# State stores moved from GpSimd's queue to SyncE's, three granules behind the update, with the values of the recurrent samples loaded two steps ahead

## The chip, the cores and the metric

The kernel runs on one core of one Trainium2 chip. The metric is the device time of one execution in microseconds; the figure for the kernel before is the median of three runs. Engines are named as in the profile: PE (TensorE matmul), PEld (its weight load), DVE (VectorE), ACT (ScalarE), POOL (GpSimd) and SP (SyncE). SP and GpSimd appear here mostly as queues from which transfers (DMAs) are issued.

## The reference, cut to what matters

One layer of a decoder trunk runs over 256 prompt tokens and 8 single-token samples, 264 columns in all. An input projection feeds three mixers (A: spatial gating, B: HGRN2, C: gated linear attention); their outputs are projected, gated, merged and projected again, and a squared-ReLU MLP follows. All of it is float32. The change touches the part of mixers B and C that belongs to the samples. Each sample has a recurrent state per head, which is read, updated by its one token and written back, and whose product with the query is the mixer's output:

```python
# per sample b and head h; B has 8 heads of 128x128, C has 4 heads of 128x256
S_new = exp(log_f)[:, None] * S_old + k[:, None] * v[None, :]   # written out
o     = S_new.T @ q                                              # used further on
```

The three groups of the kernel are heads 0 to 3 of B, heads 4 to 7 of B, and the four heads of C. Each has 8 samples, so 8 steps of four heads in B's groups and 16 steps of two heads in C's; each step's state is 256 KB.

## The kernel before, in words

The matrix work is a long row of *granules*. A granule (`granule`) takes 512 KB of weights from SP's queue (`Stream.load`, line 613), splits them into a high and a low part (`split`: ACT casts `whi` on line 109, DVE subtracts for `wlo` on line 106), and multiplies three times per weight tile (lines 656, 657, 658: `whi` by high, `whi` by low, `wlo` by high), 24 matmuls in all. Weights are loaded five granules ahead into four `raw` buffers and split two ahead into six half-granule buffers.

After each granule `background()` counts `now[0]` up by one and lets two queues of Python generators go on: `bg` (the mixers' prompt part, `mixer_r`) and `bs` (the samples' part, `samples_r`), the latter at half a step a granule. A generator yields a cost, or a condition that must hold before it goes on. Products that PE owes for either of them are gathered and issued in a *slot* (`slot`), between two granules: `levels` (line 678) for the prompts and `samples` (line 685) for the states. `Rounds.load` (line 339) loads the weights of the modulation on SP, and `Rounds.steps` (line 376) uses them.

`samples_r` goes through the steps of a group. `fetch` loads a state into one of four `st` buffers (line 1081, GpSimd), `values` loads the sample's value rows, broadcast over 128 partitions, from a small DRAM tile `vs_d` into one of two `vbc` buffers (line 1087, GpSimd). Then ACT scales the state (line 1107), DVE adds the outer product (line 1109), and GpSimd stores it (line 1110). The state stays in its buffer until the slot has used it. In step n the program issues, in this order, the fetch of step n+2, the values of step n+1, the update of step n, and its store.

What sets the order on each engine: in this stage PE's and GpSimd's instructions run in the order in which the program emits them (`manual_schedule`), while a scheduler orders those of ACT, DVE and SP beforehand and may move work ahead of its place in the program. On the chip every engine runs its own list in order, and an instruction that waits holds up all behind it on that engine.

At the group's end the rows `os_` are normalised (lines 1119 to 1121); `finish` transposes them on PE (line 1307) where the mixer's output is needed. `A1` and `A2`, `G1` and `G2` are small tiles of modulation factors, each used in a stage of its own.

Of the kernel before, what the change touches and what calls it, by code (L numbers as in the profile page):

```python
# [15 lines left out]
P = 128  # L16
D = 2048
KT = D // P
# [3 lines left out]
NC = 1 + NS  # L22
# [13 lines left out]
CHUNKS = (2, 2, 4, 4, 4)  # L36
RATES = ((1.8, 0.5), (1.6, 0.5), (1.25, 0.5), (1.0, 0.5))
ST_BUFS = 4
VB_BUFS = 2
N_PRE = 6  # L40
PRE_AT = (2, 3, 4)
ADA_BATCH = 4
# [15 lines left out]
def hybrid_step_kernel(  # L58
# [8 lines left out]
    nc = tc.nc  # L67
# [14 lines left out]
    def nm(s):  # L82
        uid[0] += 1
        return f"{s}_{uid[0]}"

    def blk(shape=None, dt=F32):
        shape = shape or [P, 4, NT]
        return blkp.tile(shape, dt, tag="b", name=nm("b"))
# [4 lines left out]
    def tmp(shape, tag, bufs=2):  # L93
        return tp.tile(shape, F32, tag=tag, name=nm(tag), bufs=bufs)

    def const(shape, name, dt=F32):
        return cp.tile(shape, dt, tag=name, name=name)

    def mul(o, a, b):
        V.tensor_tensor(o, a, b, op=ALU.mult)  # L100
# [25 lines left out]
    order = tc.manual_schedule(engines={mybir.EngineType.PE, mybir.EngineType.SP, mybir.EngineType.Pool})  # L126
# [263 lines left out]
    now = [0]  # L390
# [78 lines left out]
    A1 = const([P, KT, NC], "A1")  # L469
# [190 lines left out]
                done(acc0)  # L660
        stream[0].ahead()

    levels, samples = [], []

    def slot():

        lv = [x for x in levels if x[0] + AGE <= now[0]][:2]
        sv = [x for x in samples if x[0] + AGE <= now[0]]
        del levels[:len(lv)]
        del samples[:len(sv)]  # L670
        if lv:
            pl = sm([P, 2, 8, 32])
            for i, (_, lhs, rhs, _) in enumerate(lv):
                for h in range(4):
                    for hf in range(2):
                        for b in range(4):
                            t0 = hf * P + b * 32
                            T.matmul(pl[32 * b:32 * b + 32, i, 2 * h + hf, :], lhs[:, h, t0:t0 + 32], rhs[:, h, t0:t0 + 32], start=True, stop=True)  # L678
        if sv:
            G, qm, os_ = sv[0][1]  # L680
            nh = 512 // G.dv
            po = sm([P, G.dv])
            for h in range(4):
                for i, (_, _, b, sts) in enumerate(sv):
                    T.matmul(po[32 * h:32 * h + 32, :], qm[:, h, b, :], sts[h // nh][:, h % nh, :], start=i == 0, stop=i == len(sv) - 1)  # L685
        if rounds.due():
            rounds.steps()
        for i, (_, _, _, put) in enumerate(lv):
            put(pl[:, i])
        if sv:  # L690
            if sv[0][2] == 0:
                V.tensor_copy(os_, po)
            else:
                add(os_, os_, po)
# [3 lines left out]
    def background():  # L698

        now[0] += 1  # L700
        while later and later[0][0] < now[0]:
            later.pop(0)[1]()
        bg.pump(rate[0])
        bs.pump(rate[1])
        wait = max([now[0] + 1 - AGE - x[0] for x in levels + samples] + [0])
        if wait and any(x[1][0].i == 2 for x in samples):
            wait += 2
        if rounds.due() and (wait or now[0] >= rounds.at + rounds.pace) or wait >= SLOT_WAIT:
            slot()
        rounds.tick()  # L710
# [13 lines left out]
    def tiles(bl):  # L724
        return lambda k: moving(bl[k // 4][:, k % 4, :])

    def pair(b, g):
        return b[:, 2 * g:2 * g + 2, :]
# [57 lines left out]
    order = tc.manual_schedule(engines=set(every))  # L786
# [97 lines left out]
    def mixer_a():  # L884
# [71 lines left out]
        for gp in range(4):  # L956
# [12 lines left out]
            )  # L969
            V.scalar_tensor_tensor(u[:, :, 0:NP], yv[:, :, 0:NP], 0.5, u[:, :, 0:NP], ALU.mult, ALU.mult)  # L970
            yield
    order = tc.manual_schedule(engines={mybir.EngineType.PE, mybir.EngineType.Pool})
    order.__enter__()
    gen_a = mixer_a()
    bg.g.append(gen_a)
# [56 lines left out]
    def gla_group():  # L1032
# [30 lines left out]
        G.gates = gates  # L1063
        return G

    def samples_r(G):

        dv = G.dv
        nj, nh = dv // P, 512 // dv
        q, k, g = G.q, G.k, G.g  # L1070
        fs = tmp([P, 4, NS], "fs")
        S.activation(fs, g[:, :, NP:NT], AF.Exp)
        qm = blk([P, 4, NS, 32])
        mul(qm, q[:, :, NP:NT].unsqueeze(3).to_broadcast([P, 4, NS, 32]),
            delta.rearrange("p (b c) -> p b c", b=NS).unsqueeze(1).to_broadcast([P, 4, NS, 32]))
        steps = [(b, h) for b in range(NS) for h in range(0, 4, nh)]
        ahead, vals = [], []

        def fetch(b, h):
            st = tmp([P, nh, dv], "st", ST_BUFS)  # L1080
            nc.gpsimd.dma_start(st, G.s_in(b, h, nh))
            ahead.append((st, now[0]))

        def values(b, h):
            v = tmp([P, 4, P], "vbc", VB_BUFS)
            r0 = 4 * nj * b + h * nj
            nc.gpsimd.dma_start(v, vs_d[G.i, r0:r0 + 4, :].partition_broadcast(P))
            vals.append((v.rearrange("p (h j) v -> p h (j v)", h=nh), now[0]))

        for s in steps[0:2]:  # L1090
            fetch(*s)
            yield
        values(*steps[0])
        yield
        os_ = tmp([P, dv], f"os{G.i}", 1)
        sts = []
        for n, (b, h0) in enumerate(steps):
            if n + 2 < len(steps):

                yield lambda: len(sts) + sum(len(x[3]) for x in samples) <= ST_BUFS - 3  # L1100
                fetch(*steps[n + 2])
            if n + 1 < len(steps):
                values(*steps[n + 1])
            yield lambda: now[0] >= max(ahead[0][1] + FETCHED, vals[0][1] + FETCHED - 1)
            st, v = ahead.pop(0)[0], vals.pop(0)[0]
            for i in range(nh):
                S.activation(st[:, i, :], st[:, i, :], AF.Copy, scale=fs[:, h0 + i, b:b + 1])  # L1107
            for i in range(nh):
                V.scalar_tensor_tensor(st[:, i, :], v[:, i, :], k[:, h0 + i, NP + b:NP + b + 1], st[:, i, :], ALU.mult, ALU.add)  # L1109
            nc.gpsimd.dma_start(G.s_out(b, h0, nh), st)  # L1110
            sts.append(st)
            if h0 + nh == 4:
                samples.append((now[0], (G, qm, os_), b, sts))
                sts = []
            yield
        yield lambda: not samples
        yield READY
        ss, rr = tmp([P, 1], "sss", 1), tmp([P, 1], "srr", 1)
        S.activation(tmp([P, dv], "vt"), os_, AF.Square, accum_out=ss)
        rstd_small(ss, 1.0 / dv, rr)  # L1120
        S.activation(os_, os_, AF.Copy, scale=rr)
        G.os = os_
        yield

    def mixer_r(G):
# [18 lines left out]
        q, k, g = G.q, G.k, G.g  # L1144

        bs.g.append(samples_r(G))


# [258 lines left out]
    G1 = const([P, KT, NC], "G1")  # L1407
# [41 lines left out]
    def put_rows(m, pt, rows):  # L1449
        S.copy(in_rows(rows, 0, m), pt[:, 0])  # L1450
        V.tensor_copy(in_rows(rows, 1, m), pt[:, 1])
# [20 lines left out]
    order = tc.manual_schedule(engines={mybir.EngineType.PE})  # L1472
# [7 lines left out]
    for m in range(8):  # L1480
        if m in PRE_AT:
            n = N_PRE // len(PRE_AT)
# [8 lines left out]
            S.activation(tmp([P, 1], "srr", 1), sqacc[:, 0:1], AF.Sqrt)  # L1491
    rounds.drain()
    rounds = pre
    A2 = const([P, KT, NC], "A2")
    V.scalar_tensor_tensor(A2, mod[:, 4 * KT:5 * KT, :], 1.0, gpre2T.unsqueeze(2).to_broadcast([P, KT, NC]), ALU.add, ALU.mult)
    B2 = mod[:, 3 * KT:4 * KT, :]
    order.__exit__(None, None, None)
    order = tc.manual_schedule(engines={mybir.EngineType.PE, mybir.EngineType.DVE, mybir.EngineType.Activation})
# [35 lines left out]
    Q.tensor_tensor(xsT, xsT, gs, op=ALU.add)  # L1534
    Q.tensor_tensor(xa, xsT, A2[:, :, 1:NC], op=ALU.mult)

# [50 lines left out]
    def put_quad(q, i2, i, src, vt):  # L1587
        k = 4 * q + 2 * i2 + i
        if i == 0 and (q == 0 or i2 == 0):
            V.tensor_scalar(vt[:, i, 0:NP], src, A2[:, k, 0:1], B2[:, k, 0:1], ALU.mult, ALU.add)  # L1590
        else:
            S.activation(vt[:, i, 0:NP], src, AF.Identity, scale=A2[:, k, 0:1], bias=B2[:, k, 0:1])
        if q == 0 or i == 1:
# [6 lines left out]

    rate[:] = (0.0, 0.0)
    rounds.pace, rounds.batch = 5, 2
    G2 = const([P, KT, NC], "G2")
    h2H, h2L = tiles(h2h), tiles(h2l)

    def begin_up():
# [33 lines left out]
    def down(f, ah, al):  # L1640
        for m in range(8):
# [8 lines left out]
            if f == NFB - 1:  # L1650
                g = gated(m, dst, G2)
                later.append((now[0], lambda m=m, g=g: put_rows(m, to_tokens(g), yt)))
# [3 lines left out]
    order = tc.manual_schedule(engines={mybir.EngineType.PE})  # L1656
    order.__enter__()
    pend = up(0, zs)
    for f in range(NFB):
        nxt = up(f + 1) if f + 1 < NFB else None  # L1660
        if f == NFB - 1:
            rounds.drain()
            mul(G2, mod[:, 5 * KT:6 * KT, :], gpost2T.unsqueeze(2).to_broadcast([P, KT, NC]))
            yt = [[blk([P, 1024]) for _ in range(2)] for _ in range(2)]
# [9 lines left out]
    order = tc.manual_schedule(engines=set(every))  # L1674
# [9 lines left out]
    dst = pair(y2[3], 1)  # L1684
# [3 lines left out]
    def last_tile(i):  # L1688
# [120 lines left out]
```

## Time and profile before

| | |
|---|---|
| Median of three runs | 1823.93 us (1821.64 to 1825.94) |
| The profiled execution | 1821.87 us |
| Its span, first to last instruction | 1820.0 us |
| Mean granted TensorE clock | 0.998 |
| PE busy | 1780.2 us (98%) |
| PEld busy | 1689.8 us (93%) |
| DVE busy | 1178.7 us (65%) |
| ACT busy | 996.9 us (55%) |
| POOL busy | 136.9 us (8%) |
| DMA, mean over the span | 243 GB/s |

The states are worked on between 356 us (first fetch) and 808 us (last product of a state) of the span. In the rows shown below, a group's row gives engine, line, operation, tiles and count; a row of the timeline begins with start and duration in microseconds and ends, in brackets, with the idle time of the engine before it and what ended that; a row of waits reads "who <- for whom: us in total, times, longest". A row of windows gives the stretch, its length, then the busy time of PE, PEld, DVE, ACT and POOL with the number of instructions, then the granted clock (1.00 is full), the DMA engines' busy share and GB/s.

### The profile page before, as it was taken

How to read it: one execution, taken by the hardware profiler on the slowest of the kernel's cores; microseconds unless marked ns; L12 is line 12 of the kernel's file. 1: busy time of each engine (PE TensorE's matmuls, PEld its weight loads, DVE VectorE, ACT ScalarE, POOL GpSimd, SP SyncE). 2: the span in 40 equal slices, each digit the busy share in tenths (PEclk: the TensorE clock that was granted, in tenths of full speed). 3: DMA queues.
4: the chain of work that ended last, by engine and by line, in shares of the span. 5: the costliest groups of instructions: out<-in, count | busy, mean ns of one | idle time of the engine just before them, and what ended most of it. 6: DMA issues, size and time to landing. Idle time of an engine off the chain costs nothing.

```text
span 1820.0 us, 42083 instructions
## 1 busy us (share of the span) xinstructions
PE 1780.2 (98%) x16970; PEld 1689.8 (93%) x16970; DVE 1178.7 (65%) x2077; ACT 996.9 (55%) x1824; POOL 136.9 (8%) x228
## 2 busy tenths in 40 slices
PE   6999999999999999999999999999999999999998
PEld 4889999989988989989999989999999999999998
DVE  4666567787577696566555667555666666666666
ACT  5444364676766766654445666555554545454544
POOL 3221000102111111210000000000000000000000
PEclk9999999999999999999999999999999999999999
DMA  9987788788788789897978954777666666666663
GB/s 325 339 348 262 253 282 261 211 257 290 231 290 264 227 271 301 274 321 243 307 248 267 330 168 152 251 256 223 195 196 194 195 196 196 197 196 193 196 193 118
DMA packets 330180, 442.05 MB, mean 243 GB/s; under 512 B 14947, under 2 KB 276945, under 8 KB 329985
## 3 DMA queue, kind: packets, MB, share of 16 engines
q1 hardware_dynamic: 311872, 380.52, 65.1%
q0 software_dynamic: 17184, 57.85, 9.0%
q8 instruction: 133, 2.18, 0.5%
q10 hardware_dynamic: 928, 0.99, 0.2%
q14 instruction: 63, 0.51, 0.1%
HBM read 427.60 MB, written 11.70 MB: 241 GB/s over the span
## 4 chain that ended last, share of the span: by engine, by line
PE 88%; DVE 2%; issue 2%; DMA 1%; ACT 1%; POOL 0%; ACTq 0%; DVEq 0%; POOLq 0%
PE mm L656 27%; PE mm L658 26%; PE mm L657 26%; PE ada L376 3%; DMA vbc<-vs_d 1%; PE ada L308 1%; PE sm L854 1%; DVE wlo L106 1%; PE sm L678 1%; PE sm L685 0%; DVE b L106 0%; PE sm L1578 0%; PE sm L1209 0%; DMA st<-in_state_hgrn_dram 0%; ACT whi L109 0%
## 5 line engine op out<-in xcount | busy, mean ns | idle before, releaser
L656 PE MATMUL mm<-b,whi 128*128 128x264 f32 x4608 | 1286.9, 279 | 6.8 <-ACT whi L109 2.5
L658 PE MATMUL mm<-b,wlo 128*128 128x264 f32 x4608 | 1274.5, 277 | 5.2 <-DVE wlo L106 4.8
L657 PE MATMUL mm<-b,whi 128*128 128x264 f32 x4608 | 1273.4, 276 | 0.5 <-DVE b L106 0.4
L106 DVE TENSOR_TENSOR wlo<-raw,whi 128x512 fp32r<-128x512 f32 x1136 | 768.8, 689 | 443.8 <-ACT whi L109 442.4
L109 ACT CAST whi<-raw 128x512 fp32r<-128x512 f32 x1136 | 688.9, 616 | 626.9 <-DVE wlo L106 310.7
L656 PEld LDWEIGHTS mm<-b,whi 128*128 128x128 f32 x4608 | 872.3, 189 | 48.7 <-issue 26.4
L658 PEld LDWEIGHTS mm<-b,wlo 128*128 128x128 f32 x4608 | 872.3, 189 | 7.1 <-DVE wlo L106 7.1
L657 PEld LDWEIGHTS mm<-b,whi 128*128 128x128 f32 x4608 | 872.4, 189 | 1.1 <-DVE b L106 0.6
L103 DVE TENSOR_TENSOR b<-b,mm 128x528 f32<-128x528 f32 (+1 forms) x137 | 95.4, 698 | 63.3 <-PE mm L658 55.6
L1109 DVE SCALAR_TENSOR_TENSOR st<-vbc,b,st 128x128 f32<-128x128 f32 (+1 forms) x96 | 34.2, 392 | 52.4 <-DMA vbc<-vs_d 45.9
L1107 ACT ACTIVATE st<-st,fs 128x128 f32<-128x128 f32 (+1 forms) x96 | 37.0, 430 | 48.2 <-DMA st<-in_state_hgrn_dram 28.2
L1746 POOL TENSOR_TENSOR gs<-b,G 128x16 f32<-128x16 f32 x1 | 0.2, 222 | 714.1 <-DVE b L103 714.1
L485 POOL DMA_DIRECT2D b<-in_w_ada_dram x64 | 46.3, 725 | 48.0 <-PE ada L308 30.4
L376 PE MATMUL ada<-araw,cT 128*32 128x512 f32 x296 | 40.7, 601 | 0.0
L308 PE MATMUL ada<-b,cT 128*32 128x256 f32 (+1 forms) x640 | 35.0, 355 | 5.3 <-DMA b<-in_w_ada_dram 5.3
L100 DVE TENSOR_TENSOR b<-b,b 128x512 f32<-128x512 f32 (+1 forms) x47 | 34.0, 743 | 1.3 <-ACT b L1221 1.0
L308 PEld LDWEIGHTS ada<-b,cT 128*32 128x32 f32 x640 | 17.8, 113 | 17.4 <-DMA b<-in_w_ada_dram 9.6
L1110 POOL DMA_DIRECT2D out_dram<-st x32 | 23.5, 735 | 129.5 <-DVE st L1109 129.5
L376 PE MATMUL ada<-b,cT 128*32 128x512 f32 x216 | 26.2, 593 | 0.0
L106 DVE TENSOR_TENSOR b<-gt,b 128x528 fp32r<-128x528 f32 x32 | 22.7, 711 | 3.2
L106 DVE TENSOR_TENSOR b<-b,b 128x1056 fp32r<-128x1056 f32 (+3 forms) x21 | 20.9, 993 | 5.9 <-ACT b L109 5.9
L106 DVE TENSOR_TENSOR b<-b 128x1024 f32<-128x1024 f32 (+1 forms) x24 | 24.3, 1018 | 0.0
(360 smaller groups left out, 895.8 us busy)
## 6 DMA issues: line engine op xcount, KB each, us to landing
raw<-in_w_in_dram SPq DMA_DIRECT2D x231, 512.0 KB, 5.0
raw<-in_w_mlp_up_dram SPq DMA_DIRECT2D x128, 512.0 KB, 3.9
raw<-in_w_mlp_down_dram SPq DMA_DIRECT2D x128, 512.0 KB, 3.7
araw<-in_w_ada_dram SPq DMA_DIRECT2D x74, 512.0 KB, 5.7
b<-in_w_ada_dram SPq DMA_DIRECT2D x54, 512.0 KB, 6.4
b<-in_w_ada_dram POOLq DMA_DIRECT2D x48, 512.0 KB, 11.3
raw<-in_w_branch_dram SPq DMA_DIRECT2D x48, 512.0 KB, 4.6
raw<-in_w_out_dram SPq DMA_DIRECT2D x32, 512.0 KB, 5.1
```

Of the source, the lines that this page charges most:

```text
L100: V.tensor_tensor(o, a, b, op=ALU.mult)
L103: V.tensor_tensor(o, a, b, op=ALU.add)
L106: V.tensor_tensor(o, a, b, op=ALU.subtract)
L109: S.copy(hi, src)
L308: T.matmul(acc[32 * j:32 * j + 32, 0:n], cT[:, k, :], w[:, n * j:n * j + n], start=k == 0, stop=k == KT - 1)
L376: T.matmul(self.acc[32 * j:32 * j + 32, :], cT[:, k, :], ws[j // 2][:, j % 2 * 512:j % 2 * 512 + 512], start=k == 0, stop=k == KT - 1)
L485: queue.dma_start(w[:, i], w1[k * P:(k + 1) * P, :, self.k0 * P:(self.k0 + self.n) * P])
L656: T.matmul(o, a, xh(k + j), start=first and j == 0, stop=False)
L657: T.matmul(o, a, xl(k + j), start=False, stop=False)
L658: T.matmul(o, b, xh(k + j), start=False, stop=last and j == n - 1)
L1107: S.activation(st[:, i, :], st[:, i, :], AF.Copy, scale=fs[:, h0 + i, b:b + 1])
L1109: V.scalar_tensor_tensor(st[:, i, :], v[:, i, :], k[:, h0 + i, NP + b:NP + b + 1], st[:, i, :], ALU.mult, ALU.add)
```

## The change

The stores of the states leave GpSimd's queue. They are put on a list with the granule at which they fall due, three after the update, and `background()` issues them from SP; a fetch that needs a buffer whose store is not yet issued issues that store first. SP's order in this stage is now the program's too. Values are loaded two steps ahead like the states, right behind the state of the same step, into three `vbc` buffers; both first steps' values are loaded before the loop, which adds one step of the generator. A group's end also waits until its stores are issued. To make room, the rows of the first two groups share one tile with the third group's, and `A2` and `G2` take the tiles of `A1` and `G1`.

```diff
-VB_BUFS = 2
+STORE_LAG = 3
+VB_BUFS = 3
...
     def background():
         now[0] += 1
+        while stores and stores[0][0] <= now[0]:
+            stores[0][2]()
         while later and later[0][0] < now[0]:
...
-    order = tc.manual_schedule(engines={mybir.EngineType.PE, mybir.EngineType.Pool})
+    order = tc.manual_schedule(engines={mybir.EngineType.PE, mybir.EngineType.Pool, mybir.EngineType.SP})
...
+        def store():
+            _, dst, st = out.pop(0)
+            nc.sync.dma_start(dst, st)
+            stores.pop(0)
...
-        values(*steps[0])
-        yield
-        os_ = tmp([P, dv], f"os{G.i}", 1)
-        sts = []
+        for s in steps[0:2]:
+            values(*s)
+            yield
+        if G.i != 1:
+            os_rows.append(tmp([P, 256], "os2", 1))
+        os_ = os_rows[-1][:, G.i % 2 * P:G.i % 2 * P + dv]
+        sts, out = [], []
         for n, (b, h0) in enumerate(steps):
             if n + 2 < len(steps):
                 yield lambda: len(sts) + sum(len(x[3]) for x in samples) <= ST_BUFS - 3
+                while out and out[0][0] <= n - 2:
+                    store()
                 fetch(*steps[n + 2])
-            if n + 1 < len(steps):
-                values(*steps[n + 1])
+                values(*steps[n + 2])
...
-            nc.gpsimd.dma_start(G.s_out(b, h0, nh), st)
+            out.append((n, G.s_out(b, h0, nh), st))
+            stores.append((now[0] + STORE_LAG, n, store))
...
-        yield lambda: not samples
+        yield lambda: not samples and not out
...
-    A2 = const([P, KT, NC], "A2")
+    A2 = A1
...
-    G2 = const([P, KT, NC], "G2")
+    G2 = G1
```

More of the change, by code (lines that the diff above doesn't have):

```diff
@@ L661, in granule @@
         stream[0].ahead()
-    levels, samples = [], []
+    levels, samples, stores = [], [], []
     def slot():
@@ L1064, in gla_group @@
         return G
+    os_rows = []
     def samples_r(G):
```

## The prediction

> **What bounds the kernel now.** The page comes first, then the waits of PE in the stage that the change touches (340 to 820 us), then the places of those waits.
>
> ```profile
> span 1820.0 us, 42083 instructions
> ...
> PE 88%; DVE 2%; issue 2%; DMA 1%; ACT 1%; POOL 0%; ACTq 0%; DVEq 0%; POOLq 0%
> ```
>
> ```profile
> PE mm L658 <- DVE wlo L106: 4.6, 5, 2.8
> PE sm L678 <- issue: 2.8, 2, 2.2
> PE mm L656 <- ACT whi L109: 1.8, 1, 1.8
> PE mm L656 <- ACT att L1187: 1.3, 1, 1.3
> ```
>
> TensorE carries 88% of the chain that ended last, and the change gives it not one matmul less. Only its idle time in this stage can be won, and the second fence holds all of it: 4.6 + 2.8 + 1.8 + 1.3 = 10.5 us. PE waits there for the weights' halves (`whi` from ACT, `wlo` from DVE), so the question is what kept those two engines. Three places of PE's timeline:
>
> ```profile
> 397.58 0.38 PE L656 MATMUL mm<-b,whi 128*128 128x264 f32 x1 [1.75 <-ACT whi L109]
> ...
> 398.51 0.59 PE L658 MATMUL mm<-b,wlo 128*128 128x264 f32 x1 [0.43 <-DVE wlo L106]
> ...
> 797.48 0.50 PE L658 MATMUL mm<-b,wlo 128*128 128x264 f32 x1 [2.78 <-DVE wlo L106]
> ```
>
> At 395.83 PE ran dry for 1.75 + 0.43 = 2.18 us, at 794.70 for 2.78 us. What ACT, DVE and GpSimd did before the first:
>
> ```profile
> 396.03 0.98 ACT L1107 ACTIVATE st<-st,fs 128x128 f32<-128x128 f32 x3 [8.91 <-DMA st<-in_state_hgrn_dram]
> ...
> 396.97 0.88 DVE L1109 SCALAR_TENSOR_TENSOR st<-vbc,b,st 128x128 f32<-128x128 f32 x3 [6.11 <-DMA vbc<-vs_d]
> ```
>
> ```profile
> 359.53 0.56 POOL L1087 DMA_DIRECT2D vbc<-vs_d  x1
> 388.30 0.76 POOL L1110 DMA_DIRECT2D out_dram<-st  x1 [28.22 <-DVE st L1109]
> 389.05 0.75 POOL L1081 DMA_DIRECT2D st<-in_state_hgrn_dram  x1
> 389.80 0.55 POOL L1087 DMA_DIRECT2D vbc<-vs_d  x1
> ```
>
> GpSimd stood 28.22 us at the store of step 0, since its update was not done. Behind the store were queued the state of step 3 (issued 389.05) and the values of step 2 (389.80). ACT, in its own order, stood 8.91 us at that state, DVE 6.11 us at those values; nothing was split meanwhile, and PE ran dry. The second place, as the chain of waits shows it:
>
> ```profile
> 788.41 0.44 POOL out_dram L1110
> ...
> 789.12 2.58 DMA vbc<-vs_d
> ...
> 795.95 0.48 DVE st L1109
> ```
>
> The values of the last step left at 789.12, behind the store of the step two before, and DVE's update began at 795.95. A stall costs twice, as the windows right behind the two places show (PE busy with its count first, granted clock sixth):
>
> ```profile
> 398.20:401.70 3.50, 3.19 (x14) 3.19 (x15) 3.47 (x7) 3.15 (x6) 0.00 (x0) 0.51 0.59 166
> 401.70:405.00 3.30, 3.30 (x32) 3.30 (x31) 3.30 (x7) 3.30 (x7) 0.00 (x0) 1.00 1.03 400
> ...
> 797.60:801.00 3.40, 3.40 (x16) 3.40 (x17) 3.40 (x6) 1.76 (x3) 0.26 (x1) 0.50 0.76 223
> ```
>
> The clock is granted at half for 3.4 us after each (16 matmuls in 3.40 us, where the middle row has 32 in 3.30), which loses 1.7 us each time.
>
> **The change part by part.**
>
> *Values two steps ahead, GpSimd without stores.* In all three groups DVE waits for values:
>
> ```profile
>   DVE st L1109: 45.9, 18
> ...
> DMA to landing us min/median/max: 3.9/6.3/8.3
> ```
>
> The 45.9 us are the ceiling on DVE's side; PE felt little of it. First place: state 3 has a free buffer, and values 2 have the third one, so both leave at about 360, beside the load at 359.53. The 8.91 and the 6.11 us go. What is late next: values 3, which need the buffer of update 0, whose end releases GpSimd at 388.30. They leave then instead of 389.80, 1.5 us before today's values 2, and land at the pace of today's (389.80 to 396.97, 7.2 us) at 395.5. If the scheduler of DVE's order puts update 3 where update 2 stands today, PE restarts 1.5 us earlier than at 398.51, at 397.0, and 397.0 - 395.8 = 1.2 us of the 2.18 stay. If it puts it later, nothing stays. I take the upper bound, 1.2, since DVE's order is not in the change's hands. For the clock the bounds are 0 and 1.7; I take 0, by the row of another gap, 2.19 us long, behind which the clock stayed whole:
>
> ```profile
> 672.61 0.53 PE L678 MATMUL sm<-b 128*32 128x32 f32 x37 [2.19 <-issue]
> ```
>
> Second group, the same wait:
>
> ```profile
> 517.95 0.61 DVE L1109 SCALAR_TENSOR_TENSOR st<-vbc,b,st 128x128 f32<-128x128 f32 x2 [5.77 <-DMA vbc<-vs_d]
> ```
>
> ```profile
> 519.84 0.38 PE L658 MATMUL mm<-b,wlo 128*128 128x264 f32 x1 [0.39 <-DVE wlo L106]
> ...
> 525.33 0.38 PE L658 MATMUL mm<-b,wlo 128*128 128x264 f32 x1 [0.40 <-DVE wlo L106]
> ```
>
> 0.79 us in all; 1.5 us earlier is enough to clear both. Last place: the values of step 15 of the third group now need only update 12 and their turn behind the fetch of state 15:
>
> ```profile
> 774.96 0.88 DVE L1109 SCALAR_TENSOR_TENSOR st<-vbc,b,st 128x256 f32<-128x256 f32 x2 [0.50 <-DMA vbc<-vs_d]
> ```
>
> ```profile
> 782.93 0.57 POOL L1087 DMA_DIRECT2D vbc<-vs_d  x1
> ```
>
> Update 12 ended at 775.8, and 782.93 is where today's values 14 stand, right behind that fetch. So they can go at 782.93 instead of 789.12, 6.2 us earlier: more than the 2.78 us gap, which goes with its 1.7 us of clock.
>
> *Stores on SP, three granules behind.*
>
> ```profile
> out_dram<-st POOLq DMA_DIRECT2D x32, 256.0 KB, 5.5
> ...
> out_dram<-b SPq DMA_DIRECT2D x5, 256.0 KB, 2.3
> ```
>
> ```profile
> L613 SPq DMA_DIRECT2D raw<-in_w_in_dram x191: 367/368/842, 18.1 to 965.2; - x191
> ```
>
> ```profile
> SPq L613 <- DVE wlo L106: 257.2, 101, 8.3
> ```
>
> 32 issues at 0.368 us are 12 us of SP, which spends 257.2 us of this stage waiting for splits: hidden. Without that cover they would cost at most 12 us. Each store waits on SP for its update, and the weight loads are queued behind it. But a granule is 24 matmuls, 2.5 us at the middle row's rate, and the load ahead of the store on SP already waits for a split that comes after the update in program order; so I take 0, against up to 8.3 us, the longest that SP stands today, of which PE would feel what its split buffers do not cover. The bytes are the same; in SP's ring a store can delay the load behind it by about 2.3 us (its own landing row), within that 8.3.
>
> *SP's order by hand.* Loads of the modulation weights, which the scheduler now pulls forward, come at their place in the program. Same loads, same bytes: 0, with the extra waits inside the bound just named.
>
> *One more step before each group, and the group's end also waits for its stores.* At half a step a granule that is two granules, 5 us.
>
> ```profile
> L1121 ACTq EVENT_SEMAPHORE  x2: 17/17/17, 620.0 to 813.4; - x2
> ```
>
> ```profile
> L1307 PE MATMUL sm<-cst,os x4: 272/272/273, 633.2 to 850.8; 128*128 128x128 f32 x4
> ```
>
> The second and third group's rows are ready at 620 and 813 and are transposed at 633 and 851: 13 and 37 us of cover, 0. *Shared tiles (`A1`, `G1`, the groups' rows)*: the new writers come after the old readers in both orders, 0.
>
> The sum: 2.18 + 2.78 + 0.79 of gaps and 2 x 1.7 of clock are 9.15 us won, 1.2 given back: 7.95. The profiled execution took 1821.87 (span 1820.0), so 1813.9; the median of the runs is 1823.93, 2.06 more, so **1816**.
>
> **The rivals.**
>
> *The state is late instead (slower).* A fetch needs its buffer's old store landed. GpSimd used to store right after the update; SP does so three granules later. The third group's fetches go in pairs, and the odd one's store comes out about when the slot's matmuls do:
>
> ```profile
> ACT st L1107 <- DMA st<-in_state_gla_dram: 13.7, 8, 2.8
> ```
>
> ```profile
> 772.37 0.88 DVE L1109 SCALAR_TENSOR_TENSOR st<-vbc,b,st 128x256 f32<-128x256 f32 x2 [7.22 <-DMA vbc<-vs_d]
> ```
>
> ```profile
> 779.28 0.64 PE L685 MATMUL sm<-st,b 128*32 128x256 f32 x8
> ```
>
> ```profile
> 784.38 0.37 SPq L613 DMA_DIRECT2D raw<-in_w_in_dram  x1
> ```
>
> The update of 772.37 would be stored behind the load of 784.38, land at 787 to 790 (2.3 or 5.5 us) and hold back the next fetch, which now goes right after the slot of 779.28, by 5 to 8 us; ACT would stand at that state, and so would the values behind it. ACT's 8.91 us cost PE 2.18, so 6.7 us are covered. Today's longest wait there is 2.8; a delay over 3.9 us decides. For it: the arithmetic of this pair. Against: 784.38 is late because DVE stood 7.22 us, which goes, and the scheduler that orders ACT knows of the lag. Each such stall costs what the first place costs, 2.18 + 1.7 = 3.9 us. One leaves 4.05 us of gain (1819.9), two leave 0.15 (1823.8), three make it 3.75 us slower (1827.7), four 7.65 (1831.6).
>
> *The engines of the DMA are the limit, not the order of issue.* Then values issued earlier land no earlier, and it stays at 1823.9. Against: values take 6.3 us from issue at the median whether somebody waits or not. The Trainium skill, "DMA: Bandwidth & Descriptors", section "Issuing engines are not separate DMA queues", holds that DMAs from SP and GpSimd share the same 16 engines, so a second issuer saves only issue time; by that rule the move by itself brings nothing. The trace agrees as to the bytes, but the wait of 28.22 us stands in front of an issue.
>
> *The half clock is not the stalls' doing.* Then 3.4 us of the gain stay lost: 1823.93 - 4.55 = 1819.4. For it: no drop behind the gap of 2.19 us. Against: both drops start within 0.2 us of a gap's end. The Trainium skill, "TensorE: Matmul & The Clock Gate", section "Part 1: The HAM clock gate", has the clock halve after an idle window of about 3.4 us; by it gaps of 2.18 and 2.78 us would not do it. The trace disagrees in two of three gaps over 2 us.
>
> **How the numbers follow.** Forecast, with up to one late state: 0.57, own range 1812 to 1821. Clock not the stalls' doing 0.07. Two late states 0.10, DMA limit 0.06, three or more late states 0.20. Faster by over 0.2% (3.65 us, about what a measurement can tell) is 0.57 + 0.07 = 0.64, within it 0.16, slower 0.20. The low end is the whole 9.15 without anything given back, less the 2.3 us by which the runs' lowest lies under their median: 1812. The high end takes in three late states and 1 us of spread: 1829.
>
> **What would show it.** Right: no GpSimd store, no wait of GpSimd's loads for updates near 388 but at the fourth values; the two gaps gone or under 1.2 us; the clock whole from 390 to 810; DVE's wait for values far under 45.9 us. Wrong: GpSimd's fetches waiting for a store to land, ACT's wait for states grown past 6.7 us at a time, a new half-clock window, SP standing at a store with weight loads behind it, or the two gaps unmoved.

## The result, and the profile after

The changed kernel takes 1832.01 us (median of 6 runs, 1829.39 to 1834.14) against 1822.18 us before (6 runs): 1.005 times as long, interval 1.004 to 1.006. The forecast was 1816, the range 1812 to 1829. It came out slower, by the mechanism of the rival "the state is late instead".

The page of the changed kernel's profiled execution (1832.23 us):

```profile
span 1830.4 us, 42095 instructions
...
PE 88%; DMA 2%; ACT 2%; DVE 1%; issue 1%; POOL 0%; SPq 0%; ACTq 0%; DVEq 0%; POOLq 0%
```

All of PE's waits between 340 and 820 us, to be set against the 10.5 us of before (the lines moved: 657, 658, 659 are the three products, 1263 and 1264 the two halves of the prompt's products in `mixer_r`, 1267 ACT's scaled copy of the first half):

```profile
PE sm L1264 <- ACT b L1267: 6.0, 1, 6.0
PE mm L657 <- ACT whi L110: 3.2, 3, 2.0
PE sm L686 <- ACT b L1249: 2.0, 1, 2.0
PE mm L659 <- DVE wlo L107: 1.7, 4, 0.5
PE sm L679 <- issue: 1.6, 1, 1.6
PE mm L659 <- issue: 1.5, 1, 1.5
PE mm L657 <- issue: 1.4, 1, 1.4
PE sm L1309 <- ACT b L1311: 0.5, 1, 0.5
```

They add up to 17.9 us, 7.4 more than before. The kind has changed: of the 4.6 us for `wlo` 1.7 are left, and the largest wait, 6.0 us, is for ACT's copy of the prompt's products, which cost PE nothing before. Another copy of ACT's (line 1249) costs 2.0 us, and the wait for `whi` has grown from 1.8 to 3.2.

The windows of the changed kernel at the first of the two places of before, and at the new one:

```profile
395.00:399.00 4.00, 4.00 (x38) 4.00 (x37) 3.96 (x10) 0.62 (x2) 0.00 (x0) 1.00 0.47 123
...
727.00:734.50 7.50, 5.07 (x17) 4.53 (x18) 3.89 (x8) 3.22 (x8) 1.46 (x2) 0.55 0.58 175
```

At 395 us PE is busy throughout at the whole clock: that gap is gone. Around 727 us the clock is at half for 6.8 us. PE's timeline shows when the gain turned into a loss, by the first product of the same granule in both kernels: granule 109 of the stage starts at 667.1 us before and at 663.5 after, so the change was 3.6 us ahead by then, although it had entered the stage 1.3 us later. Granule 110 is at 673.1 and 666.3 (the kernel before stood its 2.19 us at 672 in between), granule 120 at 706.6 and 704.2, granule 125 at 728.1 and 739.3, granule 145 at 794.3 and 811.0, granule 150 at 814.1 and 824.5. The gain was made, and 20.3 us were lost between granules 109 and 145, which is where the third group's states are worked on; 6.3 us came back at the second place of before, where the changed kernel has no wait.

The chain behind the largest gap, from the timelines of DVE, SP, GpSimd, ACT and PE of the changed kernel (update of step 4 of the third group, its store, the fetch of the state four steps on, and what stands behind that state):

```profile
688.10 0.48 DVE L1123 SCALAR_TENSOR_TENSOR st<-vbc,b,st 128x256 f32<-128x256 f32 x1
...
714.70 1.38 SPq L1086 DMA_DIRECT2D out_dram<-st  x2
...
721.35 0.71 POOL L1091 DMA_DIRECT2D st<-in_state_gla_dram  x1 [13.87 <-PE mm L659]
...
724.37 0.51 ACT L1121 ACTIVATE st<-st,fs 128x256 f32<-128x256 f32 x1 [6.64 <-DMA st<-in_state_gla_dram]
...
728.55 0.82 ACT L1267 ACTIVATE b<-sm,ft 128x256 f32<-128x256 f32 x2
...
729.43 1.22 PE L1264 MATMUL sm<-b,b 128*128 128x256 f32 x2 [6.03 <-ACT b L1267]
```

The update ended at 688.6 us. Its store left SP 26.1 us later, at 714.70, since it stood at its place among the weight loads, and landed at 720.76. GpSimd took up the fetch 0.59 us after the landing, ACT stood 6.64 us at the state, the copy of the prompt's products stood behind it on ACT, and PE stood 6.03 us for the buffer that the copy empties. The row of the fetch names a matmul as releaser; PE's products of that buffer were done at 715.7, so of the fetch's conditions only the store's landing is left, and experiment `e11_constant_source` shows that it was this one.

The waits of the other engines in the same stretch, of the changed kernel:

```profile
POOL st L1091 <- DMA out_dram<-st: 48.2, 6, 20.2
...
DVE st L1123 <- DMA vbc<-vs_d: 45.7, 13, 7.8
...
ACT st L1121 <- DMA st<-in_state_gla_dram: 34.6, 8, 9.0
```

GpSimd's wait for stores to land is new, and it is larger than its row says, since most of these waits are put down to a matmul, like the one in the chain. By the times of landing, 14 of the 32 fetches start 0.56 to 0.60 us after the store of four steps before has landed, and GpSimd stood 144.1 us before them; in the kernel before there is no such fetch. ACT's wait for the third group's states has grown from 13.7 to 34.6 us and its longest from 2.8 to 9.0. DVE's wait for values, 45.9 us before, has not shrunk: the values of a step now leave right behind its state, and the state leaves late (that this is the reason is argued, not tested).

### The profile page after: what moved, and what is told of

It is laid out like the page before. It is cut to its first block, busy times and chain, and to the rows that moved or that the text cites. A ratio compares the mean times of both kernels' runs of the same rounds, so it can differ in the third digit from the quotient of the medians.

```text
span 1830.4 us, 42095 instructions
## 1 busy us (share of the span) xinstructions
PE 1783.5 (97%) x16970; PEld 1691.7 (92%) x16970; DVE 1181.5 (65%) x2076; ACT 998.1 (55%) x1824; POOL 113.0 (6%) x196
## 3 DMA queue, kind: packets, MB, share of 16 engines
q8 instruction: 133, 2.18, 0.5%
## 4 chain that ended last, share of the span: by engine, by line
PE 88%; DMA 2%; ACT 2%; DVE 1%; issue 1%; POOL 0%; SPq 0%; ACTq 0%; DVEq 0%; POOLq 0%
PE mm L657 27%; PE mm L658 26%; PE mm L659 26%; PE ada L377 3%; DMA vbc<-vs_d 1%; PE ada L309 1%; PE sm L679 1%; PE sm L857 1%; ACT whi L110 1%; DVE wlo L107 1%; DMA out_dram<-st 0%; PE sm L686 0%; PE sm L1593 0%; PE sm L1224 0%; DMA st<-in_state_gla_dram 0%
## 5 line engine op out<-in xcount | busy, mean ns | idle before, releaser
L1123 DVE SCALAR_TENSOR_TENSOR st<-vbc,b,st 128x128 f32<-128x128 f32 (+1 forms) x96 | 34.2, 390 | 55.7 <-DMA vbc<-vs_d 45.7
L1121 ACT ACTIVATE st<-st,fs 128x128 f32<-128x128 f32 (+1 forms) x96 | 36.9, 429 | 52.3 <-DMA st<-in_state_gla_dram 34.6
L309 PEld LDWEIGHTS ada<-b,cT 128*32 128x32 f32 x640 | 17.9, 114 | 17.2 <-DMA b<-in_w_ada_dram 9.1
L1647 ACT ACTIVATE b<-vt 128x528 fp32r<-128x528 f32 x32 | 22.7, 710 | 1.0
```

The costliest lines, as they stand in the source:

```text
L309: T.matmul(acc[32 * j:32 * j + 32, 0:n], cT[:, k, :], w[:, n * j:n * j + n], start=k == 0, stop=k == KT - 1)
```

## The experiments

Three theories stood against each other. Theory 1: a late store keeps the buffer, the next fetch comes late, ACT stands at the state, and PE runs dry. Theory 2: SP's order by hand, or the stores among the weight loads, cost by themselves. Theory 3: the values two steps ahead let the scheduler reshape the order of ACT and DVE. A ratio is to the kernel before, run on the same chip; its interval is in brackets.

### How long the store waits

```diff
-STORE_LAG = 3
+STORE_LAG = 1      # e1_lag1;  6 in e4_lag6
```
```diff
-            out.append((n, G.s_out(b, h0, nh), st))
-            stores.append((now[0] + STORE_LAG, n, store))
+            nc.sync.dma_start(G.s_out(b, h0, nh), st)      # e7_lag0
```

> The changed kernel with its stores one granule behind the update instead of three. Theory 1 (the lagged store lands late, so GpSimd's fetch into its buffer is late, ACT stands at the state, and PE runs dry): stores leave SP about two granules (5 us) earlier, the fetches are bound by the slot again, the 6.03 us gap of PE behind ACT in the third group and its half clock go: 1816 to 1822 us. Theory 2 (SP's order by hand, or stores among the weight loads, is what costs): nothing changes, 1829 to 1834. Theory 3 (the values two steps ahead let the scheduler pull the updates forward, and so reshape ACT's and DVE's order): 1829 to 1834 too.

> The changed kernel with its stores six granules behind the update, or at the fetch that needs the buffer, whichever comes first. Theory 1: nearly every fetch now waits for a store issued beside it, ACT's wait for states grows from 52 us to 80 or more, 1836 to 1850 us. Theory 2: the number and place of the issues on SP is much the same, 1829 to 1834. Theory 3: 1829 to 1834.

> The changed kernel with each store put on SP's queue at the update itself, no granule behind. Theory 1 (a late store makes the fetch late): as with one granule or a little better, since no fetch can wait for a store any more, 1814 to 1819 us. Rival (the lag is needed, since SP stands at the store until the update is done, with weight loads queued behind it): above 1822, with waits of SP for line 1123's update and of ACT for weights.

| lag, granules | update's end to store, mean of 32 | time | ratio |
|---|---|---|---|
| 0 | 13.7 us | 1819.97 us | 0.998 [0.997, 0.999] |
| 1 | 18.7 us | 1817.55 us | 0.998 [0.997, 0.999] |
| 3 | 25.7 us | 1832.01 us | 1.005 [1.004, 1.006] |
| 6 | 32.4 us | 1862.83 us | 1.022 [1.020, 1.024] |

The second column comes from the timelines of DVE and SP. With one granule the time came out in theory 1's range, with none 1 us above it, with six 13 us above. Up to one granule the lag is free; above, the price grows faster than the lag. With a lag of one, three fetches start right behind a store's landing, after 14.7 us of waits in all, against 14 fetches and 144.1 us with three. With six granules (the rows of GpSimd and ACT, then PE's):

```profile
POOL st L1091 <- DMA out_dram<-st: 85.9, 5, 34.0
...
ACT st L1121 <- DMA st<-in_state_gla_dram: 42.0, 12, 10.1
...
ACT st L1121 <- DMA st<-in_state_hgrn_dram: 40.3, 5, 12.4
...
PE sm L686 <- ACT b L1249: 8.8, 1, 8.8
```

The first two groups' states are late now too, and PE's idle time in the stage is 39 us. What also follows from the table: with no lag at all a store leaves 13.7 us after its update, because ACT and DVE run ahead of the program's place while SP keeps to it.

### Theory 2: SP's order, and the stores themselves

```diff
-    order = tc.manual_schedule(engines={mybir.EngineType.PE, mybir.EngineType.Pool})
+    order = tc.manual_schedule(engines={mybir.EngineType.PE, mybir.EngineType.Pool, mybir.EngineType.SP})
# e3_sp_by_hand: this edit alone, in the kernel before;
# e5_sp_scheduled: the changed kernel without this edit
```

> The kernel before with SP's order in this stage by hand and nothing else. Theory 1 and theory 3: 1820 to 1825 us, as before. Theory 2 in its first form: 1828 or more, with SP standing at loads of the modulation weights and weight loads late behind them.

> The changed kernel, three granules of lag, with SP's order in this stage left to the scheduler as before the change. Theory 1: the scheduler pulls the stores forward to their updates, whatever their place in the program, so the fetches are bound by the slot again: 1815 to 1820 us. Rival (the lag counts by its place in the program alone, or stores among the weight loads cost by themselves): 1829 to 1834.

`e3_sp_by_hand` took 1822.89 us, ratio 0.9998 [0.9988, 1.0009]: SP's order by hand costs nothing. In its trace PE's waits at the two places of before come to 0.9 and 2.8 us, with the whole clock behind both, so the size of a single gap can shift without the change, whether with SP's order or from one execution to the next. `e5_sp_scheduled` took 1818.49 us, 0.997 [0.996, 0.998], and its stores left 0.7 us behind their updates on the mean: the scheduler had put them there, whatever lag the program asked for. SP then did stand at stores, with the weight loads queued behind it:

```profile
SPq L1086 <- DVE st L1123: 28.2, 14, 4.7
```

28.2 us in 14 waits, and PE shows no wait for `whi` in the stage; the time is that of a lag of one. The prediction allowed up to 8.3 us for this wait; it cost nothing that the time shows, and the lag that avoids it is what costs.

### Theory 1, the isolating run

```diff
         def store():
             _, dst, st = out.pop(0)
-            nc.sync.dma_start(dst, st)
+            nc.sync.dma_start(dst, cst[:, 256:768].rearrange("p (h d) -> p h d", h=nh))
```

> The changed kernel, lag of three granules, with one edit: each of the 32 stores on SyncE takes its 256 KB from a constant tile instead of the state's buffer. It leaves the states' values out of the output; stores, bytes and their places on SyncE stay as they are, but no buffer of a state waits any more for a store to land. Theory 1 (a late store keeps the buffer, the fetch comes late, ScalarE stands at the state, PE runs dry): GpSimd's waits for stores (48.2 us) and nearly all of ScalarE's wait for the third group's states (34.6 us) go, the gap of 6.03 us with its 6.8 us of half clock goes or falls under 4.3, PE's idle time in the stage falls from 18.0 to 8 or under, and the time is 1815 to 1819 us, as low as with a lag of one granule or lower. Theory 2 (the stores among the weight loads of SyncE cost by their issue and bytes): nothing changes, 1829 to 1834. Theory 3 (values two steps ahead reshape ScalarE's and VectorE's order): the gap at ScalarE's copies of the prompt's products stays, over 4 us, and the time is 1825 or more.

Measured: 1819.86 us, ratio 0.998 [0.997, 0.999], that of a lag of one granule, 1 us above the expected range. The kernel leaves the states out of its output. Same number of stores, same bytes, same places on SP; only the buffers are free of them. Its waits, and the fetch of the chain above in GpSimd's timeline:

```profile
POOL st L1091 <- PE sm L686: 185.2, 10, 47.2
...
ACT st L1121 <- DMA st<-in_state_gla_dram: 19.0, 10, 5.3
```
```profile
711.08 0.71 POOL L1091 DMA_DIRECT2D st<-in_state_gla_dram  x1 [11.70 <-PE sm L686]
```

GpSimd no longer waits for a store anywhere; the fetch that stood until 721.35 leaves at 711.08, released by the slot's product. The wait for the third group's states is back to 19.0 us, as with a lag of one (18.6); theory 1 had expected nearly all of it to go. PE's idle time in the stage is 7.5 us, of which 4.2 are the gap at the copies, and 6.8 us at half clock stay there. The whole loss against a lag of one granule is therefore the buffer's wait for the store's landing, and theory 2 is out: 32 stores on SP at these very places cost nothing by themselves.

```diff
-            stores.append((now[0] + STORE_LAG, n, store))
+            stores.append((now[0] + (1 if G.i == 2 else STORE_LAG), n, store))   # e9_third_group
```

> The changed kernel with a lag of one granule in the third group alone; the first two keep three. Theory 1 as the traces place it (three of the four gaps over 2 us or over 1.5 stand in the third group, at 678, 713 and 723): 1817 to 1822 us, at least three quarters of the 14.5 us between lags three and one. If the loss is spread evenly over the three groups, or comes from the first two by way of a later start: 1826 to 1829. Theory 2: a mean of the two lags by the number of stores, 16 of 32, about 1825.

1819.77 us, 0.998 [0.997, 0.999]. A shorter lag in the third group alone brings back all of it, so at three granules the loss lies in that group.

### A fifth buffer

```diff
-NBLK = 28
+NBLK = 27          # both: a block less makes the room
-ST_BUFS = 4
+ST_BUFS = 5        # e6_five_states alone, with the lines below
...
-                yield lambda: len(sts) + sum(len(x[3]) for x in samples) <= ST_BUFS - 3
+                yield lambda: len(sts) + sum(len(x[3]) for x in samples) <= 1
-                while out and out[0][0] <= n - 2:
+                while out and out[0][0] <= n - 3:
```

> The changed kernel, three granules of lag, with a fifth buffer for states, so that a fetch needs the store of one step earlier; room for it comes from one block buffer less (27 for 28). Theory 1: the fetches no longer wait for a store's landing and reach chip as early or earlier than with one granule of lag: 8 to 15 us under its control with 27 blocks. Rival (the update pulled forward by early values costs, not the late state): within 4 us of its control.

> The changed kernel with 27 block buffers instead of 28, the control for the run with five state buffers. Either theory: 1829 to 1840 us; what it has over 1832 is the price of the block buffer.

`e6_five_states` took 1852.14 us, 1.015 [1.013, 1.017]; its control with the smaller pool of blocks 1850.27 us, 1.014 [1.013, 1.016]. The fifth buffer gained nothing, against theory 1's expectation of this run, and the control lies 10 us above its own range. GpSimd's waits for stores, in the control and with five buffers:

```profile
POOL st L1091 <- DMA out_dram<-st: 77.7, 7, 20.3
```
```profile
POOL st L1091 <- DMA out_dram<-st: 98.7, 7, 28.3
```

With one buffer more the fetches still found a store in front of them. The stores had fallen further back: 34.6 us behind their updates on the mean, against 27.2 in the control. Why they did is not settled; the lost block costs about 17 us by itself (1.014 against 1.005) and shifts everything else in the stage, so this pair does not weigh much either way.

### The last link: ACT's copy

```diff
-                S.activation(so[:, i, :], p0[:, i, :], AF.Copy, scale=ft[:, h0 + i:h0 + i + 1])
+                V.tensor_scalar(so[:, i, :], p0[:, i, :], ft[:, h0 + i:h0 + i + 1], None, ALU.mult)
# e13_products_dve: lag three;  e12_lag1_products_dve: lag one
```

> The changed kernel with its lag of three granules, and ScalarE's scaled copy of the prompt's products moved to VectorE. It tests the last link of theory 1: the wait of 6.64 us for a state reached PE only because this copy stood behind it on ScalarE. If so, the gap of 6.03 us at 723 goes with its 6.8 us of half clock (3.4 us lost), while ScalarE's waits for the states (34.6 us) stay: 1832.0 - 9.4 = 1822.6, so 1821 to 1826 us. If PE was held by anything else that stands behind the state (the splits of the weights, the update on VectorE): a gap of 4 us or more stays within some us of 723, and the time is 1829 to 1834.

> The changed kernel with a lag of one granule, and ScalarE's scaled copy of the prompt's products (which empties PE's buffer p0) moved to VectorE, which adds to the same tile right behind it. Theory 1 and 3 together: what is left at a lag of one is the gap of 3.47 us at these copies, which stand behind states on ScalarE, with 3.4 us of half clock (1.7 us lost); both go: 1817.55 - 5.2 = 1812.4, so 1811 to 1815 us. If VectorE, which waits for the values and the scaled states too, is as late at the copy as ScalarE was: 1817 to 1819, with the gap at the same matmuls and VectorE as releaser.

Both missed: 1836.92 us, 1.007 [1.005, 1.009], and 1819.83 us, 0.998 [0.996, 0.999], no better than without the edit. The gap stayed at the same matmul (7.4 and 4.8 us), and DVE was the releaser. DVE's timeline with a lag of three:

```profile
724.66 0.48 DVE L1123 SCALAR_TENSOR_TENSOR st<-vbc,b,st 128x256 f32<-128x256 f32 x1 [7.66 <-ACT st L1121]
...
728.41 0.87 DVE L1267 TENSOR_SCALAR b<-sm,ft 128x256 f32<-128x256 f32 x2
```

The late state holds both engines: ACT waits for it, DVE for ACT's scaled state, and the copy stands behind it in either list. The copy was where the delay reached PE, not its cause; moving it moves nothing.

### The halves of the change apart, and the gap that is left

Where the values are two ahead and hardly a fetch waits for a store (lags of none and one, SP's order left to the scheduler, the constant source), a gap of 3.5 to 4.2 us still stands between 715 and 723 us at these copies; the kernel before has none there. Four runs on that and on the halves of the change:

```diff
-            out.append((n, G.s_out(b, h0, nh), st))
-            stores.append((now[0] + STORE_LAG, n, store))
+            nc.gpsimd.dma_start(G.s_out(b, h0, nh), st)     # e2_pool_stores: values two ahead alone
```
```diff
-VB_BUFS = 3
+VB_BUFS = 2        # e14_one_ahead_lag1, e15_one_ahead_lag3: stores on SP, values one ahead
...
-                values(*steps[n + 2])
+            if n + 1 < len(steps):
+                values(*steps[n + 1])
```
```diff
-FETCHED = 3
+FETCHED = 5        # e16_later_use: lag one; a state is scaled five granules behind its fetch
```

> The changed kernel with its stores back on GpSimd, right behind the update as before; values stay two steps ahead in three buffers, SP's order stays by hand. Theory 1: no fetch waits for a late store; GpSimd waits for updates again, but values are a step further ahead, so the old gaps at 396 and 795 are at most half: 1816 to 1821 us. Theory 2 in its first form (SP's order by hand): 1829 to 1834; in its second (stores among the loads): 1816 to 1821. Theory 3: 1829 to 1834.

> Stores on SyncE with a lag of one granule, but the values one step ahead in two buffers, as before the change: the stores' part alone, without its late landing. Theory 3's remnant (values two ahead bring ScalarE's and VectorE's order into the shape in which the copies of the prompt's products stand behind a state): the gap of 3.5 us near 716 is absent, and the gap near 396 of the kernel before, or its like, is back; the sum leaves it at 1819 to 1823 us. If the gap near 716 comes from the four buffers of the states (a fetch waits for the slot of four steps before, whatever the values do), it is there too, over 3 us: 1820 to 1825.

> Stores on SyncE with a lag of three granules, the values one step ahead in two buffers. Theory 1: the lag alone does the harm, whatever the values do, so this stands 10 to 17 us above its twin with a lag of one granule: 1830 to 1838 us, with GpSimd's waits for stores at 40 us or more and ScalarE's waits for the third group's states over 30. If the late state hurts only where the values too are ahead (the updates are then pulled further forward from their place, and the lag in time grows): within 5 us of its twin, 1820 to 1827.

> The changed kernel with a lag of one granule, and with each state scaled at least five granules behind its fetch in the program in place of three. If the place in the program decides which comes first on ScalarE: the copies of the prompt's products come ahead of the state near 716, the gap of 3.47 us and its half clock go, 1812 to 1816 us. If the scheduler orders ScalarE by its own estimate of when the state is there: the gap stays, 1816 to 1820. If the later use holds buffers longer, so that fetches come later: over 1822, with GpSimd's waits for slots grown past 181 us.

| | stores | values | time | ratio |
|---|---|---|---|---|
| `e2_pool_stores` | GpSimd, at the update | two ahead | 1822.46 us | 1.000 [0.999, 1.001] |
| `e14_one_ahead_lag1` | SP, lag 1 | one ahead | 1814.90 us | 0.996 [0.994, 0.997] |
| `e15_one_ahead_lag3` | SP, lag 3 | one ahead | 1835.56 us | 1.008 [1.005, 1.011] |
| `e16_later_use` | SP, lag 1, later use | two ahead | 1814.31 us | 0.996 [0.994, 0.997] |

`e15_one_ahead_lag3` and `e16_later_use` came out in a range that was expected; `e2_pool_stores` lies 1.5 us above theory 1's range and far under the other two theories', and `e14_one_ahead_lag1` 4 us under its lowest.

*Values two ahead alone* bring no time, and GpSimd still stands at its stores:

```profile
POOL out_dram L1124 <- DVE st L1123: 86.0, 9, 27.7
...
PE sm L1263 <- ACT b L1266: 4.3, 1, 4.3
...
PE sm L679 <- issue: 2.1, 1, 2.1
...
PE mm L659 <- DVE wlo L107: 1.7, 3, 0.7
```

Yet the two gaps of before are not the reason. The first is down from 2.18 to 1.14 us (0.45 and 0.69, at 397 and 398 us) with the whole clock, and the second is gone. In their place stand the gap at the copies (4.27 us at 723) and one of 2.07 us at 541, each with a window of half clock behind it, so that PE's idle time in the stage comes to the 10.5 us of before again.

*Stores on SP alone* bring the gain. Here is the first place again, GpSimd's timeline with the values one ahead, and the windows behind it:

```profile
360.89 0.75 POOL L1091 DMA_DIRECT2D st<-in_state_hgrn_dram  x1
389.11 0.55 POOL L1097 DMA_DIRECT2D vbc<-vs_d  x1 [27.48 <-DVE st L1123]
```
```profile
394.00:399.00 5.00, 5.00 (x47) 5.00 (x46) 4.97 (x10) 1.92 (x4) 0.00 (x0) 1.00 0.55 160
```

The values of step 2 leave at 389.11, hardly earlier than before the change (389.80), and PE still doesn't run dry: that state 3 left at 360.89 and not at 389.05 was enough. The last place is not won by this half: a gap of 1.90 us stands at 787, with a window of half clock behind it. *A lag of three without the values ahead* costs 20.7 us against its twin, above the 10 to 17 expected; GpSimd waits 134.8 us for stores there, and the worst gap (6.8 us) is at another place, 433 us, for `whi` in the first group. Its stores leave 18.0 us behind their updates on the mean, no more than the 18.7 us of `e1_lag1`, so the mean alone does not tell; that 16 of its fetches start right behind a store's landing, after 207.7 us of waits, does. The lag harms by itself, and where it reaches PE depends on what happens to stand behind a late state.

*The gap near 716 us* is an order on ACT. ACT's timeline with a lag of one, then the same with the later use:

```profile
715.12 0.51 ACT L1121 ACTIVATE st<-st,fs 128x256 f32<-128x256 f32 x1 [4.52 <-DMA st<-in_state_gla_dram]
...
718.86 0.82 ACT L1267 ACTIVATE b<-sm,ft 128x256 f32<-128x256 f32 x2
```
```profile
713.35 0.84 ACT L1267 ACTIVATE b<-sm,ft 128x256 f32<-128x256 f32 x2 [0.79 <-PE sm L1263]
...
720.62 0.51 ACT L1121 ACTIVATE st<-st,fs 128x256 f32<-128x256 f32 x1 [2.92 <-DMA st<-in_state_gla_dram]
```

With the state scaled two granules further on in the program, the copies come first, and the gap is gone, as it is with the values one ahead. That supports theory 3 for this one gap; it is worth 3.5 us and a half clock of 3.4 us, of which some came back elsewhere. `e14_one_ahead_lag1` and `e16_later_use` beat the kernel before by 0.4%. Their intervals just overlap that of `e1_lag1` (0.9966 to 0.9987), so that they also beat the plain lag of one is likely and not certain.

## Why the prediction was wrong, point by point

- *The two gaps of before.* Right. Both are gone, as are those at 519 and 525 us; at the second place 6.3 us came back, against the 2.78 and 1.7 of the sum. The halves of the change show what won each place: `e14_one_ahead_lag1` wins the first place with the values as before, so there it was enough that no fetch is queued behind a store on GpSimd (SP's order by hand, which these runs share, may have a part in it: alone it left 0.9 us there), and `e2_pool_stores` wins the last with the values ahead. That `e2_pool_stores` gains no time all the same is the doing of two other gaps. Of the 1.2 us that were to stay at the first place nothing stayed.
- *Stores on SP at 0.* This is the step that failed: three granules of lag were put at 0 in the sum, and against a lag of one they cost 14.5 us (1832.01 and 1817.55). The issue cost was right (`e11_constant_source`), and SP standing at a store cost nothing that shows (`e5_sp_scheduled`); what was mis-sized is how late the lag makes the store. The prediction's only figure for a granule was 2.5 us, its bare matmuls, which makes 7.5 us for three. The 140 granules from 311.0 to 811.0 us took 3.57 us each, and the time from an update to its store was 25.7 us on the mean, because the updates run ahead of their place in the program by some 14 us (the 13.7 us at lag 0) and the stores don't. The landing of 5.6 us at the median comes on top.
- *The rival of the late state.* Right as a mechanism: fetches wait for landings, ACT's wait passed 6.7 us (9.0 at the longest), a new half-clock window came. Its worked example came near: ACT's wait of 9.0 us is that of the same pair of fetches, but it was the store of the third group's step 10 that held them, not that of step 11, and PE stood 2.02 us behind it at 782. It priced a stall at 3.9 us; the largest cost 6.03 us and 6.8 us at half clock, 9.4 us together. Three or four stalls were to give 1827.7 to 1831.6, and 1832.0 was measured; since the stalls were of other sizes than priced, that nearness is luck.
- *The arguments against that rival* fell. "The scheduler that orders ACT knows of the lag": the list of ACT put the state ahead of the copy that PE was waiting for. DVE's stand of 7.22 us, which was to go: DVE still stood up to 7.8 us at values.
- *DVE's wait for values "far under 45.9"*: wrong, 45.7. It is 20.7 at lag 0 and 33.9 with the constant source, but 34.2 in `e13_products_dve` too, where the states are late, so what sets it stays open.
- *SP's order by hand at 0*: right.
- *The DMA engines as the limit*: out, since moving the store's time alone moved the kernel by 45 us between lags of one and six. The move gained with a lag of one, since what it took from GpSimd's queue was a wait. By the Trainium skill, "DMA: Bandwidth & Descriptors", section "Issuing engines are not separate DMA queues", a second issuer saves issue time alone. The bytes did land no faster (5.6 us for a store after, 5.5 before), but the gain is more than that rule gives.
- *The extra step and the shared tiles at 0*: not tried by themselves; they are in the kernel with a lag of one, which gains 0.2% with them. The 4.9 us that it gains (1817.55 against 1822.46) are still under the 7.95 of the sum, which had no term for the gap at the copies (3.47 us, and 1.7 of clock).
- *The half clock.* Right that it follows the stalls, wrong on which: the last section.

In the sum: 7.4 us more of idle time in the stage and 1.7 us more lost to half clock (10.2 us of half clock in place of 6.8), and the later entry of 1.3 us, make 10.4; the spans differ by 10.4. Nothing shows the later entry to be the change's doing: with a lag of one the stage begins 0.2 us earlier than before.

## What to carry to other kernels

A store moved to a queue that keeps the program's order was late here by the whole distance between the program's place and the engine's real position, on top of the granules written in the code; read that distance from a trace before costing the lag. A buffer's cycle is update, store, landing, fetch, landing: a delay at one point cost nothing here until it used up the slack of the cycle, and then it came out on whatever instruction stood behind the late buffer in an in-order list. Taking a blocking store out of a load queue was worth 0.2 to 0.4% here, with any lag that stayed under that slack.

## What the runs showed of the hardware

In these traces the granted clock is decided in fixed windows, and what counts is how much of a window PE is idle. In all 17 traces the changes of the clock lie whole multiples of 3.413 us apart, to within 0.2 us. Cut into these windows, those at the full clock that begin after 30 us of the span (8,847) give: after every window with over 2.0 us of idle PE (39 of them) the next one is granted at half; after none with under 1.7 us; between the two both happen. In the first 30 us it is otherwise: at 26 to 27 us half clock followed five windows with 1.2 to 1.6 us of idle PE, and why stays open. The prediction took the 2.19 us gap near 672 us, after which the clock stayed whole, as a row against the stalls. The windows of the kernel before show where the two differ: its first gap, then that one, cut at the limits of the windows:

```profile
394.83:398.24 3.41, 1.49 (x11) 1.10 (x10) 1.27 (x4) 2.21 (x6) 0.00 (x0) 1.00 0.52 191
667.90:671.31 3.41, 2.52 (x47) 2.28 (x45) 0.51 (x2) 2.28 (x5) 0.00 (x0) 1.00 0.99 335
671.31:674.72 3.41, 2.11 (x51) 2.07 (x52) 3.41 (x7) 1.81 (x4) 0.00 (x0) 1.00 0.90 310
```

The first gap fell into one window (1.49 us busy, 1.92 idle), the other was split by a limit into 0.9 and 1.3 us. In the changed kernel (PE alone) two gaps of the same 2.0 us part in the same way:

```profile
710.62:714.03 3.41, 2.37 (x22) 1.00 0.91 298
714.03:717.44 3.41, 2.43 (x24) 1.00 0.96 331
782.30:785.71 3.41, 1.06 (x7) 1.00 0.36 142
```

The first two rows hold the gap of 2.01 us near 713, split, with the whole clock behind it; the third holds that of 2.02 us at 782.3, in one window, with half clock from 785.7. The Trainium skill, "TensorE: Matmul & The Clock Gate", section "Part 1: The HAM clock gate", calls the window free-running and 3413 ns long; the traces agree. That it takes an idle window to halve the clock, which the prediction read as 3.4 us without work, is met here with 2.0 us of the window idle. So a gap of 2.0 to 2.2 us cost 1.7 us of clock or nothing here, by where it fell, and a price for it carries that much chance.
